# Eight columns of one tile for the index of late V rows, in place of two buffers, in a decoder trunk with PEER layers

## The chip, the cores and the metric

The kernel runs on one core of one Trainium2 chip. The metric is the device time of one execution in microseconds; before the change it is 3107.72 us, the median of three runs (3106.04 to 3110.53). Engines are named as in the profile: PE is TensorE (PEld its weight loads), DVE is VectorE, ACT is ScalarE, POOL is GpSimd, SP is SyncE.

## The reference

Four decoder layers over 256 tokens of width 1024. Each layer is a token mixer (HGRN2, FoX attention, Mamba-2 SSD, HGRN2) followed by a PEER feed-forward layer, and each adds to the residual stream. The part around the change is the PEER layer, which picks 16 of 16384 single-neuron experts for each token and each of 8 heads:

```python
def peer_ffn(h, w_q, sub_keys, u_tab, v_tab):
    ...
    idx = jnp.take_along_axis(cand_i, pos, axis=-1)     # 16 experts per token and head
    gates = jax.nn.softmax(top_s, axis=-1)
    u = jnp.take(u_tab, idx, axis=0)
    v = jnp.take(v_tab, idx, axis=0)
    act = jax.nn.gelu(jnp.einsum('md,mhkd->mhk', xb, u), approximate=False) * gates
    return jnp.einsum('mhk,mhkd->md', act, v)
```

So each expert costs a row of U (4 KB), a dot product with the token, a GELU, and a row of V (4 KB) that is added with the weight `act`.

## The kernel before

**Stages and steps.** Tokens are handled in blocks of 128, so there are 8 stages (4 layers, 2 blocks). A stage has 64 steps, one for each of 8 heads and 8 pairs of experts; the 512 steps of the program are counted by `i`. One step takes two experts of each of the block's 128 tokens, in two groups of 128 rows: group `g` = 0 is the first 64 tokens, group 1 the other 64. Beside the steps of stage s runs, spread over them as background work, all that stage s+1 needs first: its norm, its mixer's projections, its queries and scores (`side`, `products_`, `others`), and the routing of the heads to come (`route_steps`). The order on every engine is that in which the code is written; nothing is reordered.

**A step's transfers.** All are indirect DMAs that POOL issues, on one queue, with 128 row numbers each, a column of an int32 tile:
- `fetch(i, 0)` (L1588) brings the U and V rows of group 0, 8 KB each, 1 MB in all, into one of four buffers.
- `fetch(i, 1)` (L1588) brings the U rows of group 1 alone, 0.5 MB, into one of three buffers.
- `rest_of(i)` (L1600) brings the V rows of group 1 later, 0.5 MB into another three buffers, and only for tokens whose GELU is not exactly zero: row numbers beyond the table are left out by `bounds_check`. These are the late V rows.

The row numbers of the late V rows are made by DVE in `ask(i)`: one operation sets a large offset where the GELU is zero, and the next writes the column `w` of 128 int32 numbers, the tile `ask`. That tile had two buffers used in turn, so `ask(i)` writes where `ask(i-2)` wrote, and may do so only when the DMA `rest_of(i-2)` has read its row numbers; what the program waits for is that DMA's end.

**A step's order.** In step i, POOL issues `fetch(i+2, 1)`, `rest_of(i-1)` and `fetch(i+3, 0)` (a little apart from this at the ends of stages). DVE does `dot(i, 0)` and `dot(i, 1)` (the scalar_tensor_tensor of 128x1024 with a sum), then DVE's share of the background work, then `ask(i)`, then routing and more background work. ACT does the GELUs and the 64-column diagonals `dg` and `dh`, by which PE weighs the rows. PE's `add_rows` (L1668) in step i adds first the late V rows of step i-3, with `dh`, then the V rows of group 0 of step i, with `dg`; behind them stand the background matmuls (L258, L262).

**Who frees what.** `fetch(i+4, 0)` needs the buffer that `dot(i, 0)` and `add_rows` of (i, 0) have read. `fetch(i+3, 1)` needs that of `dot(i, 1)`. `rest_of(i)` needs the numbers of `ask(i)` and the buffer that `add_rows` of step i-3 has read. Besides, the software DMAs use eight semaphores in turn (DMASW0 to DMASW7), and each DMA waits until the one eight before it has landed. SP issues the weights' loads (L412, 1 MB each, on a queue of its own), partly into the two buffers of the tile `raw`.

Helpers: every DVE operation carries L219 or its own line, ACT's carry L232, matmuls L258, transposes L262; the trace's groups are therefore told apart by their tiles.

Of the kernel before, what the change touches and what calls it, by code (L numbers as in the profile page):

```python
# [12 lines left out]
I32 = mybir.dt.int32  # L13
# [6 lines left out]
P = 128  # L20
# [160 lines left out]
def trunk(ctx: ExitStack, tc: tile.TileContext, d: dict, out: bass.AP):  # L181
    nc = tc.nc
    SB = bass.MemoryType.PSUM
    cpool = ctx.enter_context(tc.tile_pool(name="c", bufs=1))
    rawp = ctx.enter_context(tc.tile_pool(name="raw", bufs=NRAW))
    wk2 = ctx.enter_context(tc.tile_pool(name="wk2", bufs=2))
# [58 lines left out]
    small = cpool.tile([P, 2], F32, name="eps")  # L245
    eps, spare = small[:, 0:1], small[:, 1:2]
    trimask = cpool.tile([P, P], U8, name="trimask")
    m64 = cpool.tile([P, 64], F32, name="m64")

    pe = [0.0]  # L250
# [104 lines left out]
    for l in range(DEPTH):  # L355
# [9 lines left out]
        for u in ours:  # L365
            t, _, i, where, again = kept[u]
# [1193 lines left out]
    acts = {}  # L1560
    accs = {}
    asks = {}
# [28 lines left out]
    def ask(i):  # L1591

        s, hh, q = pairs[i]
        a, w = acts[i], asks.setdefault(i, wk2.tile([P, 1], I32, name="ask", bufs=2))
        vec.tensor_scalar(a[:, 5:6], a[:, 3:4], 0.0, float(FAR), op0=OP.is_equal, op1=OP.mult)
        stt(w, a[:, 5:6], 1.0, got[s, hh][1][:, 1, 0, q:q + 1], op0=OP.add, op1=OP.add)

# [188 lines left out]
    for s in range(STAGES):  # L1786
# [23 lines left out]
        for i in range(64 * s, 64 * s + 64):  # L1810
# [21 lines left out]
            if i < CLOSE:  # L1832
                ask(i)
# [34 lines left out]
```

## Time and profile before

| | |
|---|---|
| median of three runs | 3107.72 us (3106.04 to 3110.53) |
| the profiled execution, its own time | 3110.88 us |
| its span | 3109.1 us |
| mean granted TensorE clock | 0.969 |
| busy share of the span: PE, DVE, POOL, ACT | 88%, 71%, 56%, 49% |
| bytes moved by DMA | 1235.74 MB, mean 397 GB/s |

The span is from the first to the last instruction of the profiled execution; 1.8 us of its own time lie around it. A row of the page's fifth part tells line, engine, operation, tiles written and read and the count, then the busy time, the mean of one in ns, and the engine's idle time just before with what ended it. In the view of windows, a row gives for a stretch of time the busy us of each engine (with its instructions), the granted clock, the mean busy share of the 16 DMA engines, and the GB/s; the DMA share goes a little over 1 where packets of an engine overlap. In the view of waits, a row names who waited, after `<-` who ended the wait, then the total in us, the number of waits and the longest.

### The profile page before, as it was taken

The numbers are of one execution on the slowest core, as the hardware profiler recorded it, in microseconds if no ns is written. First come the engines' busy times: TensorE is split into PE (matmuls) and PEld (weight loads), VectorE is DVE, ScalarE is ACT, GpSimd is POOL, SyncE is SP. The second block draws the span as 40 slices with busy tenths as digits, with TensorE's granted clock in tenths as the row PEclk, the third lists the DMA queues.
The fourth block names the chain that finished last, engine by engine and source line by source line (L and its number), as shares of the span: only waits on it lengthen the run. The fifth ranks groups of instructions, "written<-read, shape, count | busy, mean of one in ns | idle before, by whom it ended". The sixth has DMA issues, their size and how long they took to land.

```text
span 3109.1 us, 35708 instructions
## 1 busy us (share of the span) xinstructions
PE 2744.5 (88%) x9490; PEld 1110.9 (36%) x9490; DVE 2209.5 (71%) x6666; ACT 1524.9 (49%) x4410; POOL 1735.6 (56%) x1544
## 2 busy tenths in 40 slices
PE   9989897988789888999789999889988899887777
PEld 4434333332235334344233543343323253342111
DVE  1676667767866867888677787678667767787774
ACT  2455444464444644587345675346444545444333
POOL 0365465655656655555465554556546555666664
PEclk9999999999999999999999999999999999999999
DMA  7799999999999999999999999999999999999998
GB/s 310 276 408 391 407 413 413 413 409 402 409 412 414 406 412 412 380 416 411 408 391 387 382 416 415 405 396 391 416 416 407 387 394 416 393 405 397 406 411 345
DMA packets 249463, 1235.74 MB, mean 397 GB/s; under 512 B 35985, under 2 KB 36625, under 8 KB 160560
## 3 DMA queue, kind: packets, MB, share of 16 engines
q0 software_dynamic: 221184, 1039.92, 83.7%
q1 hardware_dynamic: 28080, 193.55, 15.1%
q8 instruction: 78, 1.28, 0.2%
q14 instruction: 121, 0.99, 0.1%
HBM read 1266.23 MB, written 1.05 MB: 408 GB/s over the span
## 4 chain that ended last, share of the span: by engine, by line
DMA 38%; PE 28%; DVE 21%; ACT 7%; issue 5%; POOL 0%; POOLq 0%; DVEq 0%; SPq 0%; ACTq 0%
DMA arena<-in_uv,ask 37%; PE pj L258 13%; PE pj L1668 11%; DVE arena L219 11%; PE ps L258 3%; ACT L232 3%; DVE cs L219 2%; ACT dots L232 1%; DVE si L219 1%; ACT dg L232 1%; DVE ti L219 1%; DVE af L219 1%; DVE gs L219 1%; DVE ts L219 1%; DVE ask L219 1%
## 5 line engine op out<-in xcount | busy, mean ns | idle before, releaser
L1588 POOL DMA_INDIRECT arena<-in_uv,ix x1024 | 1120.3, 1094 | 602.3 <-DVE arena L219 224.2
L219 DVE SCALAR_TENSOR_TENSOR arena<-arena 128x1024 f32<-128x1024 f32 (+3 forms) x1282 | 1285.3, 1043 | 2.8 <-DMA arena<-in_uv,ix 1.4
L1668 PE MATMUL pj<-arena,dg 128*64 128x512 f32 x2048 | 1035.3, 630 | 211.6 <-ACT dg L232 210.0
L1668 PE MATMUL pj<-arena,dh 128*64 128x512 f32 x2048 | 1028.6, 627 | 122.8 <-DMA arena<-in_uv,ask 116.3
L1600 POOL DMA_INDIRECT arena<-in_uv,ask x508 | 606.4, 1194 | 748.6 <-issue 330.5
L232 ACT ACTIVATE dots<-dots 128x1 f32<-128x1 f32 x1024 | 204.7, 200 | 1314.3 <-DVE arena L219 1312.9
L258 PE MATMUL pj<-arena 128*128 128x128 f32 (+1 forms) x1752 | 509.4, 439 | 1.8 <-ACT arena L232 0.8
L1668 PEld LDWEIGHTS pj<-arena,dh 128*64 128x64 f32 x2048 | 247.8, 141 | 652.6 <-issue 491.5
L219 DVE SCALAR_TENSOR_TENSOR ask<-dots,gs 128x1 int32<-128x1 f32 x508 | 81.0, 159 | 561.1 <-DMA arena<-in_uv,ask 551.5
L1668 PEld LDWEIGHTS pj<-arena,dg 128*64 128x64 f32 x2048 | 245.2, 139 | 628.6 <-ACT dg L232 421.1
L232 ACT ACT_TABLE_LOAD x332 | 426.0, 1283 | 6.3 <-DVE arena L219 0.8
L258 PE MATMUL pj<-raw,arena 128*128 128x512 f32 x808 | 387.3, 614 | 10.1 <-DMA raw<-in_ssm 5.1
L258 PEld LDWEIGHTS pj<-arena 128*128 128x128 f32 x1752 | 258.1, 192 | 258.8 <-issue 237.1
L258 PEld LDWEIGHTS pj<-raw,arena 128*128 128x128 f32 x808 | 144.1, 192 | 243.1 <-issue 213.3
L232 ACT ACTIVATE dg<-dg,dots 128x64 f32<-128x64 f32 x512 | 178.1, 348 | 16.6
L232 ACT ACTIVATE dg<-m,gs 128x64 f32<-128x64 f32 x512 | 170.1, 332 | 0.0
L232 ACT ACTIVATE dh<-m,dots 128x64 f32<-128x64 f32 x508 | 168.8, 332 | 1.6 <-PE pj L1668 1.6
L219 DVE TENSOR_SCALAR dots<-dots 128x1 f32<-128x1 f32 x508 | 76.6, 151 | 129.0 <-ACT dots L232 128.7
L232 ACT ACTIVATE dots<-dots,gs 128x1 f32<-128x1 f32 x508 | 149.6, 294 | 16.5
L258 PE MATMUL ps<-arena 128*128 128x128 f32 (+6 forms) x1120 | 147.4, 285 | 3.1 <-ACT arena L1252 1.3
L258 PEld LDWEIGHTS ps<-arena 128*128 128x128 f32 (+3 forms) x1120 | 111.7, 168 | 79.0 <-issue 43.2
L219 DVE DVE_READ_ACCUMULATOR arena<-arena 128x1 f32 x1024 | 83.4, 81 | 0.0
(130 smaller groups left out, 1763.3 us busy)
## 6 DMA issues: line engine op xcount, KB each, us to landing
raw<-in_ssm SPq DMA_DIRECT2D x48, 1024.0 KB, 8.9
raw<-in_hg SPq DMA_DIRECT2D x35, 1024.0 KB, 9.1
arena<-in_wq SPq DMA_DIRECT2D x28, 1024.0 KB, 8.9
arena<-in_hg SPq DMA_DIRECT2D x27, 1024.0 KB, 14.1
arena<-in_uv,ix POOLq DMA_INDIRECT x1028, 9.9
raw<-in_fox SPq DMA_DIRECT2D x14, 1024.0 KB, 9.2
arena<-in_fox SPq DMA_DIRECT2D x9, 1024.0 KB, 12.3
raw<-in_wq SPq DMA_DIRECT2D x8, 1024.0 KB, 9.9
```

The costliest lines, as they stand in the source:

```text
L219: return getattr(nc.vector, name)(o, *a, **k)
L232: nc.scalar.activation(o, i, f, **k)
L258: nc.tensor.matmul(o, w, m, start=start, stop=stop)
L1588: nc.gpsimd.indirect_dma_start(buffer(i, g), None, halved if apart(i, g) else d["uv"], bass.IndirectOffsetOnAxis(ap=got[s, hh][0][:, g, q: ...
L1600: nc.gpsimd.indirect_dma_start(rows(i, 1), None, halved, bass.IndirectOffsetOnAxis(ap=asks.pop(i), axis=0), bounds_check=2 * DEPTH * P * P ...
L1668: nc.tensor.matmul(accs[s][e][g * 64:g * 64 + 64], diags[i, g], rows(i, g)[:, e * 512:(e + 1) * 512], start=False, stop=hh == 7 and q == N ...
```

## The change

The tile `ask` becomes one tile of 128x8 int32 that lives as long as the program, and `ask(i)` writes column i mod 8 of it. `rest_of` is as it was and reads that column.

```diff
--- before.py
+++ after.py
@@ -245,6 +245,7 @@
     small = cpool.tile([P, 2], F32, name="eps")
     eps, spare = small[:, 0:1], small[:, 1:2]
     trimask = cpool.tile([P, P], U8, name="trimask")
+    index_ring = cpool.tile([P, 8], I32, name="ask")
     m64 = cpool.tile([P, 64], F32, name="m64")
 
     pe = [0.0]
@@ -1591,7 +1592,7 @@
     def ask(i):
 
         s, hh, q = pairs[i]
-        a, w = acts[i], asks.setdefault(i, wk2.tile([P, 1], I32, name="ask", bufs=2))
+        a, w = acts[i], asks.setdefault(i, index_ring[:, i % 8:i % 8 + 1])
         vec.tensor_scalar(a[:, 5:6], a[:, 3:4], 0.0, float(FAR), op0=OP.is_equal, op1=OP.mult)
         stt(w, a[:, 5:6], 1.0, got[s, hh][1][:, 1, 0, q:q + 1], op0=OP.add, op1=OP.add)
 
```

The instructions of every engine and their order stay the same; lines below the new one move by one (L1588 is L1589 after, L1600 is L1601). What moves is waits. On DVE, near the end of the last stage (two steps without background work), before:

```order
L219 SCALAR_TENSOR_TENSOR arena,dots<-arena 128x1024 [waits DMASW5_49]
L219 SCALAR_TENSOR_TENSOR arena,dots<-arena 128x1024 [waits DMASW6_49]
L219 TENSOR_SCALAR dots<-dots 128x1 [waits Activation_49]
L219 SCALAR_TENSOR_TENSOR ask<-dots,gs 128x1 [waits DMASW2_49,DVE_49]
L219 SCALAR_TENSOR_TENSOR arena,dots<-arena 128x1024 [waits DMASW0_49]
L219 SCALAR_TENSOR_TENSOR arena,dots<-arena 128x1024 [waits DMASW1_49]
L219 TENSOR_SCALAR dots<-dots 128x1 [waits Activation_49]
L219 SCALAR_TENSOR_TENSOR ask<-dots,gs 128x1 [waits DMASW5_49,DVE_49]
```

and now, at the same place:

```order
L219 SCALAR_TENSOR_TENSOR arena,dots<-arena 128x1024 [waits DMASW5_49]
L219 SCALAR_TENSOR_TENSOR arena,dots<-arena 128x1024 [waits DMASW6_49]
L219 TENSOR_SCALAR dots<-dots 128x1 [waits Activation_49]
L219 SCALAR_TENSOR_TENSOR ask<-dots,gs 128x1 [waits DVE_49]
L219 SCALAR_TENSOR_TENSOR arena,dots<-arena 128x1024 [waits DMASW0_49]
L219 SCALAR_TENSOR_TENSOR arena,dots<-arena 128x1024 [waits DMASW1_49]
L219 TENSOR_SCALAR dots<-dots 128x1 [waits Activation_49]
L219 SCALAR_TENSOR_TENSOR ask<-dots,gs 128x1 [waits DVE_49]
```

The wait for a DMA (here the ones counted by DMASW2 and DMASW5) is gone from `ask`, in 506 of its 508 instructions; the first two never had it. No DVE instruction has a wait that it did not have. In the turn of eight, the two dots behind the first `ask` wait for DMASW0 and DMASW1, the two transfers issued just ahead of the one that `ask` waited for (DMASW2). On POOL, the same place, before:

```order
L1600 DMA arena<-in_uv,ask 128x1024 [waits DMASW2_49,DVE_49,PE_49]
L1588 DMA arena<-in_uv,ix 128x2048 [waits DMASW3_49,PE_49]
L1588 DMA arena<-in_uv,ix 128x1024 [waits DMASW4_49,DVE_49]
L1600 DMA arena<-in_uv,ask 128x1024 [waits DMASW5_49,DVE_49,PE_49]
L1588 DMA arena<-in_uv,ix 128x2048 [waits DMASW6_49,PE_49]
L1588 DMA arena<-in_uv,ix 128x1024 [waits DMASW7_49,DVE_49]
```

and now:

```order
L1601 DMA arena<-in_uv,ask 128x1024 [waits DMASW2_49,DVE_49,PE_49]
L1589 DMA arena<-in_uv,ix 128x2048 [waits DMASW3_49,PE_49]
L1589 DMA arena<-in_uv,ix 128x1024 [waits DMASW4_49,DVE_49]
L1601 DMA arena<-in_uv,ask 128x1024 [waits DMASW5_49,DVE_49,PE_49]
L1589 DMA arena<-in_uv,ix 128x2048 [waits DMASW6_49,PE_49]
L1589 DMA arena<-in_uv,ix 128x1024 [waits DMASW7_49,DVE_49]
```

Nothing moved here but the line numbers: the late V rows still wait for the DMA of the same semaphore eight issues before, for DVE's `ask`, and for PE, which must have read the buffer's last rows. On PE seven waits are named otherwise, at transposes and small matmuls of the mixers; on ACT and SP nothing differs.

## The prediction

> **What bounds the kernel now.** I read the page's DMA part first, then its chain, then windows over the span, then the waits, and last a stretch of the timeline. From the page:
>
> ```profile
> DMA packets 249463, 1235.74 MB, mean 397 GB/s; under 512 B 35985, under 2 KB 36625, under 8 KB 160560
> q0 software_dynamic: 221184, 1039.92, 83.7%
> q1 hardware_dynamic: 28080, 193.55, 15.1%
> ...
> DMA 38%; PE 28%; DVE 21%; ACT 7%; issue 5%; POOL 0%; POOLq 0%; DVEq 0%; SPq 0%; ACTq 0%
> DMA arena<-in_uv,ask 37%; PE pj L258 13%; PE pj L1668 11%; DVE arena L219 11%; PE ps L258 3%; ACT L232 3%; DVE cs L219 2%; ACT dots L232 1%; DVE si L219 1%; ACT dg L232 1%; DVE ti L219 1%; DVE af L219 1%; DVE gs L219 1%; DVE ts L219 1%; DVE ask L219 1%
> ```
>
> The 16 DMA engines are busy 99% of the span (83.7 + 15.1% and a little), and 37% of the chain that ended last runs through the late V rows, whose end lets `ask` go on. These two read differently: the first says that bytes bound the kernel, the second that a loop of waits does. The windows decide between them. Row by row: most of the program, the last steps, a stretch heavy with weights, then the nine stretches between 200 and 3080 us that fall furthest behind.
>
> ```profile
> 110.00:3085.00 2975.00, 2625.42 (x9070) 1050.65 (x9068) 2177.43 (x6589) 1483.93 (x4326) 1730.96 (x1536) 0.97 1.01 404
> ...
> 3000.00:3070.00 70.00, 55.31 (x119) 14.06 (x119) 38.28 (x91) 22.33 (x89) 44.73 (x44) 0.98 1.02 414
> 1900.00:1960.00 60.00, 48.34 (x117) 16.53 (x116) 33.92 (x104) 18.60 (x55) 24.73 (x22) 0.96 1.02 417
> 235.00:265.00 30.00, 30.00 (x167) 18.18 (x166) 23.21 (x70) 14.44 (x48) 17.89 (x17) 1.00 0.97 357
> 1270.00:1315.00 45.00, 45.00 (x154) 18.18 (x154) 40.72 (x136) 27.55 (x79) 26.46 (x23) 1.00 0.95 357
> 1545.00:1585.00 40.00, 38.10 (x125) 14.99 (x124) 28.13 (x86) 16.31 (x53) 23.75 (x23) 0.99 0.97 368
> 1625.00:1665.00 40.00, 33.52 (x138) 13.08 (x135) 31.39 (x89) 21.06 (x64) 24.89 (x23) 0.96 0.94 352
> 1715.00:1755.00 40.00, 40.00 (x221) 24.36 (x218) 26.48 (x86) 17.50 (x58) 20.68 (x18) 0.94 0.94 350
> 2075.00:2120.00 45.00, 43.48 (x133) 17.11 (x130) 37.92 (x108) 32.79 (x82) 30.01 (x25) 0.96 0.94 350
> 2410.00:2450.00 40.00, 32.62 (x94) 11.11 (x93) 33.96 (x97) 20.95 (x60) 25.47 (x22) 0.96 0.96 359
> 2495.00:2530.00 35.00, 35.00 (x209) 21.68 (x207) 19.62 (x47) 17.61 (x57) 21.95 (x20) 1.00 0.98 379
> 2670.00:2712.00 42.00, 40.16 (x124) 14.24 (x124) 29.10 (x84) 18.95 (x65) 26.92 (x25) 0.96 0.98 376
> ```
>
> In the last steps, where nothing but the steps themselves runs, the DMA engines do 414 GB/s at a share of 1.02, and with weights beside them 417. Over 2975 us the mean is 404 GB/s. If all of it went at 414, 2975 x (1 - 404/414) = 72 us would go: that is the room for any change that moves no byte less. Counted by the share instead, 2975 x (1 - 1.01/1.02) = 29 us. The nine stretches last 357 us and hold 46 us of it by GB/s (for each, its length x (1 - GB/s / 414): 4.1, 6.2, 4.4, 6.0, 6.2, 7.0, 5.3, 3.0, 3.9). In seven of them PE is busy 95% or more; in two (1625 and 2410) it is 84 and 82%, and DVE 78 and 85%. So the kernel is bound by bytes nearly everywhere, and by PE or DVE in short stretches in which the queue runs low.
>
> The waits, in total:
>
> ```profile
> DVE ask L219 <- DMA arena<-in_uv,ask: 551.5, 253, 8.1
> ...
> POOL arena L1600 <- issue: 330.5, 196, 8.3
> POOL arena L1600 <- PE pj L1668: 240.6, 238, 6.6
> ...
> PE pj L1668 <- ACT dg L232: 210.0, 149, 3.2
> ```
>
> DVE's longest wait is the one that the change takes away: 253 times, 2.2 us each. The timeline near the end shows a step in that state:
>
> ```profile
> 3068.66 0.16 DVE L219 SCALAR_TENSOR_TENSOR ask<-dots,gs 128x1 int32<-128x1 f32 x1 [2.02 <-DMA arena<-in_uv,ask]
> 3068.70 1.90 PE L1668 MATMUL pj<-arena,dh 128*64 128x512 f32 x4 [1.03 <-DMA arena<-in_uv,ask]
> 3068.74 1.22 DVE L219 SCALAR_TENSOR_TENSOR arena<-arena 128x1024 f32<-128x1024 f32 x1
> 3069.59 1.24 POOL L1600 DMA_INDIRECT arena<-in_uv,ask  x1 [1.15 <-issue]
> ...
> 3073.70 0.16 DVE L219 SCALAR_TENSOR_TENSOR ask<-dots,gs 128x1 int32<-128x1 f32 x1 [2.17 <-DMA arena<-in_uv,ask]
> ...
> 3079.96 0.16 DVE L219 SCALAR_TENSOR_TENSOR ask<-dots,gs 128x1 int32<-128x1 f32 x1 [3.38 <-DMA arena<-in_uv,ask]
> ...
> 3080.89 1.30 POOL L1600 DMA_INDIRECT arena<-in_uv,ask  x1 [0.49 <-DVE ix L219]
> ```
>
> The late rows of two steps ago land; DVE's `ask` and PE's `add_rows` are let go at once; POOL issues the next late rows 0.93 us after `ask` began (3069.59 - 3068.66). The step takes 5.04 us (3073.70 - 3068.66), which is 2 MB at 414 GB/s: the wait is the queue's back pressure, felt on DVE.
>
> **The change part by part.** No instruction comes, goes or moves; 506 waits go, and no DVE or POOL instruction gains one. The writing of a column of eight in place of a column of one is the same 128x1 write, so I cost it at nothing; were each of the 508 rows of `ask` (0.16 us above) half as long again, that is 41 us of DVE, which has 2975 - 2177 = 798 us free there.
>
> *In the stretches bound by bytes* (all but some 400 us) the wait goes and its time doesn't. What is late next: the two dots wait for the transfers of DMASW0 and DMASW1, issued just ahead of the one that `ask` waited for (DMASW2). A transfer of 128x1024 f32 is 0.52 MB, 1.27 us at 414 GB/s, so DVE is held again at most 1.3 us earlier in the queue, plus the work that stood between. On POOL, the late rows then wait for the DMA eight before, two transfers ahead of the old one (2.5 us), so with the 0.93 us they can be issued up to 3.4 us earlier, and the fetches behind them too: 3.4 us x 414 GB/s = 1.4 MB more lie in the queue. The engines move the same bytes at the same rate; gain 0.
>
> *Where DVE lets the queue run low* (1625 and 2410), that deeper queue lasts 3.4 us longer. Each stretch loses more than that (6.0 and 5.3), so 2 x 3.4 = 6.8 us come back. This is an upper value if the stretch before it was not in the waiting state.
>
> *Where PE does* (the seven others), late rows hang on PE's `add_rows`, not on `ask` (the row of 240.6 us). PE gains only what it gets ahead beforehand: its wait for `dg`, 210.0 us in 149 times, 1.4 us each, which ends earlier because the dot behind `ask` starts earlier. That wait isn't there before every stretch (149 of 512 steps), so I take half: 7 x 0.7 = 4.9 us; bounds 0 and 7 x 3.4 = 23.8.
>
> *The small dips elsewhere* hold 72 - 46 = 26 us by GB/s, but part of that is the rate of skipped and short rows, which no wait explains; I take a tenth, 2.6 us, bounds 0 and 13 (half).
>
> *The end.* The last late rows are issued at 3080.89, after an `ask` that waited 3.38 us. Everything after that is a tail of add, norm and store. Issued earlier, they still lie behind other transfers; I take 2 us, bounds 0 and 3.4.
>
> *The start*, up to 110 us, has no `ask`: 0.
>
> Sum: 6.8 + 4.9 + 2.6 + 2 = 16.3 us, on the profiled execution 3110.9 - 16.3 = 3094.6; the median of the runs is 3.2 us below that execution, so 3107.7 - 16.3, or 3091 us (0.5% less). The upper bounds together give 6.8 + 23.8 + 13 + 3.4 = 47 us; all of them at once is unlikely.
>
> [...]
>
> **The rivals.**
>
> *No change (within 0.2%, 6.2 us).* The stretches are PE's, PE gains no lead, and the two of DVE are entered without a lead: only the end and some dips remain, 2 to 5 us, 3104 us. For it: seven of nine stretches have PE at 95% or more. Against: the 210 us of `dg` waits stand on PE.
>
> *A deeper queue is also faster.* At 417 GB/s where weights lie beside the V rows and 414 where they don't, more bytes in flight may raise the rate: 2975 x 404 x (1/414 - 1/417) = 20.9 us beyond the forecast, 3107.7 - 16.3 - 20.9 = 3070 us. Against: those are larger, contiguous rows. [...] The trace shows no window above 417.
>
> *Slower: the weights come late.* With 1.4 MB more of V rows ahead, a weight load that shares the engines lands up to 3.4 us later. The rows of the tile `raw`, through which most weights pass:
>
> ```profile
> L412 SPq DMA_DIRECT2D raw<-in_ssm x48: 327/328/430, 1204.7 to 1929.7; - x48
> L412 SPq DMA_DIRECT2D raw<-in_hg x35: 327/328/430, 27.1 to 2629.9; - x35
> L412 SPq DMA_DIRECT2D raw<-in_fox x14: 327/328/443, 478.5 to 1058.3; - x14
> L412 SPq DMA_DIRECT2D raw<-in_wq x8: 328/375/432, 100.1 to 2637.5; - x8
> ...
>   DMA raw<-in_ssm: 11.4, 11
> ...
>   DMA raw<-in_hg: 5.7, 3
> ...
> DMA to landing us min/median/max: 7.1/9.1/26.7
> ```
>
> PE and its weight loads wait for them 17.1 us in 14 places, so they come just in time there; there are 105 loads (48, 35, 14, 8). It decides from the point at which loads in PE's seven stretches (277 us of 2975, so about 10 of the 105) and in as many dense places again are late by the whole 3.4 us: 20 x 3.4 = 68 us less the 16.3, which is 52 us slower, 3159 us. If it is only those 14 places, 14 x 3.4 = 48 us, less 16.3: 3139 us. Against: PE, not DMA, sets the pace there, and the V rows' queue moves 83.7 of the 99% before the change too, so a load shares the engines with it already. [...]
>
> That the waits stay is excluded: the built order shows them gone.
>
> **How the numbers follow.** Forecast 0.61, at 3091 us; no change 0.22, at 3104; deeper and faster 0.11, at 3070; slower 0.06, at 3139. Two runs of this kernel differ by up to 0.14% (3106.04 to 3110.53), so about 0.2% can be told. The forecast itself reaches from 3079 (dips and PE stretches at half their bounds: 6.8 + 11.9 + 6.5 + 3.4 = 28.6) to 3101 (DVE's stretches alone). With most of the case of no change above and the half of the fast case below, the range is 3074 to 3106. Faster 0.61 + 0.11 = 0.72, same 0.22, slower 0.06.
>
> **What would show it.** Right: the wait of `ask` for the late rows gone from DVE; a new wait of the dots on `arena<-in_uv,ix`, far below 551.5 us; late rows issued earlier against the landing before them; the GB/s of 3000 to 3070 unchanged near 414, those of 1625 and 2410 up, those with PE at 100% up less. Wrong: the nine stretches as low as before (no lead was carried in), 417 or more in the last steps (depth makes speed), or PE's waits for `raw` grown from 17 us to 50 or more (weights late). The forecast's own step most likely to fail is the 3.4 us of lead: it needs POOL to be free to issue and PE to have read the buffer.

## The result, and the profile after

The changed kernel takes 3076.74 us (median of 6 runs, 3073.28 to 3080.45), the kernel before 3106.88 us beside it (6 runs, 3102.78 to 3110.78): a ratio of 0.9904, 95% interval 0.9891 to 0.9917, or 30.1 us less. The profiled execution took 3075.86 us; its span of 3074.1 us is 35.0 us shorter than that of before. The forecast was 16.3 us less, so the sign was right and the size about half. Measured again beside later experiments, the change gave 0.9905 (0.9889 to 0.9922).

From the page of the changed kernel, its DMA line and its chain:

```profile
DMA packets 249460, 1235.72 MB, mean 402 GB/s; under 512 B 35985, under 2 KB 36625, under 8 KB 160560
...
DMA 43%; PE 28%; DVE 16%; ACT 3%; issue 3%; POOL 1%; POOLq 0%; DVEq 0%; ACTq 0%
DMA arena<-in_uv,ix 23%; DMA arena<-in_uv,ask 21%; PE pj L1669 12%; PE pj L259 12%; DVE arena L219 9%; PE ps L259 3%; DVE cs L219 1%; ACT L232 1%; ACT dots L232 1%; PE ps L263 1%; DVE ti L219 1%; DVE si L219 1%; DVE ts L219 1%; DVE ask L219 1%; DVE sv L219 1%
```

The bytes are the same. The chain has 5 points more of DMA and 5 less of DVE, the late V rows (`ask`) have 16 points less, and the first fetches (`ix`) have 23, where they had at most 1.

The same windows as before, in the order most of the program, last steps, stretch with weights, nine stretches; the stretches are placed where the same steps run now, 5 to 30 us earlier, and the last steps 35 us earlier. After a window and its length stand the busy us of PE, PEld, DVE, ACT and POOL, then the granted clock, the DMA share and the GB/s:

```profile
110.00:3050.00 2940.00, 2406.96 (x9062) 1049.18 (x9061) 2218.12 (x6586) 1484.45 (x4323) 1749.17 (x1536) 0.92 1.01 409
2965.00:3035.00 70.00, 40.69 (x115) 13.98 (x112) 40.57 (x87) 21.90 (x86) 47.25 (x43) 0.78 1.02 414
1900.00:1960.00 60.00, 38.69 (x103) 15.28 (x104) 34.15 (x91) 20.42 (x65) 30.17 (x26) 0.80 1.02 416
230.00:258.00 28.00, 28.00 (x156) 16.70 (x155) 22.89 (x66) 13.76 (x46) 16.89 (x15) 1.00 1.02 413
1262.00:1306.00 44.00, 44.00 (x139) 17.05 (x136) 41.25 (x140) 28.08 (x81) 27.52 (x24) 1.00 0.97 357
1534.00:1574.00 40.00, 37.96 (x118) 14.42 (x116) 29.03 (x89) 16.82 (x53) 25.28 (x25) 1.00 1.00 393
1610.00:1650.00 40.00, 33.28 (x117) 11.94 (x114) 33.93 (x94) 22.57 (x70) 26.28 (x24) 1.00 0.96 372
1696.00:1736.00 40.00, 40.00 (x224) 24.00 (x221) 27.92 (x90) 18.49 (x60) 21.88 (x19) 0.97 0.99 389
2054.00:2098.00 44.00, 42.49 (x129) 16.62 (x128) 37.87 (x109) 32.58 (x77) 30.49 (x26) 1.00 1.00 385
2385.00:2425.00 40.00, 32.97 (x94) 11.59 (x93) 31.80 (x93) 23.32 (x64) 24.82 (x23) 0.96 0.98 380
2467.00:2502.00 35.00, 35.00 (x221) 22.63 (x219) 20.86 (x55) 16.73 (x52) 23.58 (x21) 1.00 1.02 413
2640.00:2681.00 41.00, 37.93 (x131) 14.84 (x131) 29.87 (x85) 15.72 (x57) 27.33 (x25) 1.00 1.02 409
```

Where bytes bind, nothing moved: 414 GB/s in the last steps, as before, and 416 beside the weights, where it was 417. In the stretches much came back. By the measure of the prediction, length x (1 - GB/s / 414), the room in the nine is now 0.1, 6.1, 2.0, 4.1, 2.4, 3.1, 3.3, 0.1 and 0.5, in sum 21.6 us where it was 46.0. The room of the whole row is 2940 x (1 - 409/414) = 35.5 us where it was 71.9. So of 36.4 us that came back, 24.4 did in the nine stretches and 12 elsewhere. (Window edges are whole us, so a single stretch is good to about 1 us; the GB/s of the whole row are whole numbers, so the 12 is good to some 5.)

The waits of the changed kernel:

```profile
PE pj L1669 <- DMA arena<-in_uv,ask: 451.2, 224, 9.7
DVE arena L219 <- DMA arena<-in_uv,ix: 440.2, 256, 5.4
...
POOL arena L1601 <- PE pj L1669: 257.2, 205, 5.0
...
POOL arena L1601 <- DMA arena<-in_uv,ix: 153.8, 92, 4.1
...
POOL arena L1589 <- DVE arena L219: 93.8, 131, 3.8
...
PE pj L1669 <- ACT dg L232: 39.6, 28, 2.8
```

The 551.5 us of `ask` are gone, and the dots wait 440.2 us for their own rows instead. PE waits 39.6 us for the diagonal `dg` where it waited 210.0, and 451.2 us for the late V rows themselves (116.3 before), which come when the queue has brought them.

What this does to a step is seen near 1510 us, in two neighbouring steps (236 before, 237 now), in each of which PE had to wait for late rows. Before:

```profile
1513.21 0.16 DVE L219 SCALAR_TENSOR_TENSOR ask<-dots,gs 128x1 int32<-128x1 f32 x1 [5.99 <-DMA arena<-in_uv,ask]
...
1513.26 1.90 PE L1668 MATMUL pj<-arena,dh 128*64 128x512 f32 x4 [1.37 <-DMA arena<-in_uv,ask]
...
1515.12 1.21 DVE L219 SCALAR_TENSOR_TENSOR arena<-arena 128x1024 f32<-128x1024 f32 x1
...
1516.60 0.35 ACT L232 ACTIVATE dg<-dg,dots 128x64 f32<-128x64 f32 x1
...
1517.00 1.93 PE L1668 MATMUL pj<-arena,dg 128*64 128x512 f32 x4 [1.84 <-ACT dg L232]
```

And now:

```profile
1507.25 1.21 DVE L219 SCALAR_TENSOR_TENSOR arena<-arena 128x1024 f32<-128x1024 f32 x1
...
1508.73 0.35 ACT L232 ACTIVATE dg<-dg,dots 128x64 f32<-128x64 f32 x1
...
1509.84 0.61 PE L1669 MATMUL pj<-arena,dh 128*64 128x512 f32 x1 [1.42 <-DMA arena<-in_uv,ask]
1509.96 0.61 PE L1669 MATMUL pj<-arena,dg 128*64 128x512 f32 x1
...
1511.27 0.59 PE L1669 MATMUL pj<-arena,dg 128*64 128x512 f32 x1
```

Before, the landing (1513.2) let DVE go; the first dot came 1.9 us later, ACT's `dg` after it, and PE added the late rows (1.90 us), sat idle 1.84 us, and added group 0 (1.93 us): done at 1518.93, 5.7 us after the landing. Now the dot and `dg` are done when the rows land, and PE runs both additions at once: done at 1511.86, 2.0 us after the landing. The two write different halves of the accumulator's partitions. In these rows they run beside each other: started 0.12 us apart, the eight matmuls take 2.02 us (1511.86 - 1509.84), where four took 1.90 and 1.93. That the halves are what lets them, no run shows.

Over the program, the busy time in `add_rows` alone, PE's and then PEld's, of before and of after (in the view of windows, restricted to that line):

```profile
0.00:3109.10 3109.10, 1548.11 (x4096) 420.79 (x4096) 0.97 0.99 397
```

```profile
0.00:3074.10 3074.10, 1320.11 (x4096) 414.76 (x4096) 0.93 1.00 402
```

By the groups of before, `dg` took 1035.3 us and `dh` 1028.6:

```profile
L1668 PE MATMUL pj<-arena,dg 128*64 128x512 f32 x2048 | 1035.3, 630 | 211.6 <-ACT dg L232 210.0
L1668 PE MATMUL pj<-arena,dh 128*64 128x512 f32 x2048 | 1028.6, 627 | 122.8 <-DMA arena<-in_uv,ask 116.3 <-ACT dh L232 6.2
```

So 1035.3 + 1028.6 - 1548.1 = 516 us of them ran beside each other. After, the groups `dg` and `dh` take 1126.6 and 1122.3 us, and 1126.6 + 1122.3 - 1320.1 = 929 us do.

### The profile page after: what moved, and what is told of

The parts are those of the page before. It is cut to its first block, busy times and chain, and to the rows that moved or that the text cites. A ratio compares the mean times of both kernels' runs of the same rounds, so it can differ in the third digit from the quotient of the medians.

```text
span 3074.1 us, 35204 instructions
## 1 busy us (share of the span) xinstructions
PE 2525.9 (82%) x9490; PEld 1109.9 (36%) x9490; DVE 2250.9 (73%) x6666; ACT 1526.2 (50%) x4410; POOL 1755.1 (57%) x1544
## 4 chain that ended last, share of the span: by engine, by line
DMA 43%; PE 28%; DVE 16%; ACT 3%; issue 3%; POOL 1%; POOLq 0%; DVEq 0%; ACTq 0%
DMA arena<-in_uv,ix 23%; DMA arena<-in_uv,ask 21%; PE pj L1669 12%; PE pj L259 12%; DVE arena L219 9%; PE ps L259 3%; DVE cs L219 1%; ACT L232 1%; ACT dots L232 1%; PE ps L263 1%; DVE ti L219 1%; DVE si L219 1%; DVE ts L219 1%; DVE ask L219 1%; DVE sv L219 1%
## 5 line engine op out<-in xcount | busy, mean ns | idle before, releaser
L219 DVE SCALAR_TENSOR_TENSOR arena<-arena 128x1024 f32<-128x1024 f32 (+3 forms) x1282 | 1305.5, 1046 | 449.5 <-DMA arena<-in_uv,ix 440.2
L1669 PE MATMUL pj<-arena,dh 128*64 128x512 f32 x2048 | 1122.3, 676 | 497.0 <-DMA arena<-in_uv,ask 451.2
L1589 POOL DMA_INDIRECT arena<-in_uv,ix x1024 | 1089.7, 1064 | 640.1 <-issue 160.2
L1669 PE MATMUL pj<-arena,dg 128*64 128x512 f32 x2048 | 1126.6, 678 | 31.7 <-ACT dg L232 31.5
L1601 POOL DMA_INDIRECT arena<-in_uv,ask x508 | 656.4, 1292 | 657.9 <-PE pj L1669 257.2
L1669 PEld LDWEIGHTS pj<-arena,dh 128*64 128x64 f32 x2048 | 260.6, 148 | 1078.7 <-issue 515.4
L1669 PEld LDWEIGHTS pj<-arena,dg 128*64 128x64 f32 x2048 | 261.4, 149 | 165.6 <-issue 81.5
L219 DVE MAX8 sv<-arena 128x8 f32<-128x128 f32 x256 | 61.3, 280 | 31.5 <-ACT arena L1239 17.9
```

What stands on the lines that cost most here:

```text
L219: return getattr(nc.vector, name)(o, *a, **k)
L1589: nc.gpsimd.indirect_dma_start(buffer(i, g), None, halved if apart(i, g) else d["uv"], bass.IndirectOffsetOnAxis(ap=got[s, hh][0][:, g, q: ...
L1601: nc.gpsimd.indirect_dma_start(rows(i, 1), None, halved, bass.IndirectOffsetOnAxis(ap=asks.pop(i), axis=0), bounds_check=2 * DEPTH * P * P ...
L1669: nc.tensor.matmul(accs[s][e][g * 64:g * 64 + 64], diags[i, g], rows(i, g)[:, e * 512:(e + 1) * 512], start=False, stop=hh == 7 and q == N ...
```

## The experiments

The theory of the prediction was a deeper queue of V rows (POOL issues earlier), with a little lead for PE beside it. The rivals to be told from it: that the column layout itself matters; that the gain is in proportion to the wait removed, wherever it stood; and that it is DVE's own lead that counts, and not POOL's. All ratios are to the kernel before on the same chip; the diffs are against the changed kernel.

**Two columns and three.**

```diff
-index_ring[:, i % 8:i % 8 + 1]
+index_ring[:, i % 2:i % 2 + 1]      # e1; in e2: i % 3
```

> The index columns lie in one tile, but only two of its columns are used in turn, so that ask(i) waits for rest_of(i-2) again (506 waits are back). Theory (the gain is a lead: with the wait gone, DVE and POOL run ahead and the queue is deeper when PE or DVE slow down): the wait is all there was to it, so the time of the kernel before, ratio 0.998 to 1.002, and the wait of ask for the late rows near 550 us again. Rival (the columns of one tile that is never released, in place of buffers of a pool, matter by themselves): faster than before, ratio 0.990 to 0.997.

> Three columns in turn in place of eight: ask(i) waits for rest_of(i-3), which the buffer of the late rows waits for on POOL anyway. Lead theory: that wait is one transfer (1.3 us) behind what the dots of the same step waited for, so little stands in its way: ratio 0.989 to 0.993, as with eight, and a small wait of ask, under 60 us. Rival (DVE profits from being able to run several steps ahead): only part of the gain, ratio 0.994 to 0.998.

Measured: two columns 1.0002 (0.999 to 1.0014), three 0.9907 (0.9881 to 0.9932). The wait of `ask` with two columns, then with three:

```profile
DVE ask L219 <- DMA arena<-in_uv,ask: 536.9, 242, 8.4
```

```profile
DVE ask L219 <- DMA arena<-in_uv,ask: 34.8, 34, 2.2
```

One tile with two columns is the kernel before again, so the layout costs and gives nothing and the wait is all. A third column takes the wait down to 34.8 us and gives the whole gain.

**Where the wait matters.** Eight columns only in the 159 steps around and ahead of the stretches (e3), or only in the others (e4).

```diff
+NEAR = ((8, 26), (187, 207), (228, 276), (313, 333), (372, 404), (414, 435))
+n = 8 if any(a <= i < b for a, b in NEAR) else 2      # e4: 2 and 8 swapped
-index_ring[:, i % 8:i % 8 + 1]
+index_ring[:, i % n:i % n + 1]
```

> Eight columns only in 159 of the 508 steps, namely in those of the nine stretches in which the DMA rate is low and some 10 steps ahead of each; two columns in the other 349. Lead theory: nearly the whole gain, 24 to 31 us, ratio 0.990 to 0.9925, since the lead is built up in a few steps and is used in these stretches alone. Rival (each wait that goes saves a little, in proportion to the waits taken away): these steps hold 166 of the 561 us of DVE's waits at ask, so 9 us, ratio 0.997.

> The opposite: eight columns in the 349 steps far from the nine stretches, two columns in the 159 steps in and ahead of them. Lead theory: the lead that is built up is lost at the first ask with a wait and isn't there in the stretches; what is left is the small dips and the end, 2 to 8 us, ratio 0.9975 to 0.9995. Rival (in proportion to the waits taken away): these steps hold 395 of the 561 us of waits, so 21 us, ratio 0.993.

Measured: near 0.9925 (0.9898 to 0.9952), far 0.9984 (0.9973 to 0.9996). The shares of the wait in these expectations were wrong: added up by step, the trace of before has 135.8 us of the 551.5 in the near steps and 415.7 in the others, so a gain in proportion would have been 7.4 us near (0.9976) and 22.7 us far (0.9927). The runs show the reverse, 23 us and 5 us. What was left of the wait, near and far:

```profile
DVE ask L220 <- DMA arena<-in_uv,ask: 399.5, 181, 7.6
```

```profile
DVE ask L220 <- DMA arena<-in_uv,ask: 146.5, 58, 7.8
```

399.5 us of the wait may stay and three quarters of the gain are there. What a wait is worth is decided by the stretch it stands in or ahead of. Less busy time of PE alone decides as little: its busy time in `add_rows` is 1498.7 us with the near steps free and 1390.5 with the far ones (1548.1 before), and the run that saves more of it gains less.

**Whose lead: DVE's or POOL's.** A clearing of the column that the late rows of step i-2 were fetched by waits for their landing. It is put on DVE behind `ask` (e5), or on POOL ahead of the late rows' issue (e7); e6 and e8 clear a column that is long free, so nothing waits.

```diff
 stt(w, a[:, 5:6], 1.0, got[s, hh][1][:, 1, 0, q:q + 1], op0=OP.add, op1=OP.add)
+k = (i + 6) % 8                                # e6: (i + 2) % 8, e8: (i + 4) % 8
+nc.vector.memset(index_ring[:, k:k + 1], 0)    # e7, e8: nc.gpsimd, in rest_of
```

> Eight columns, but right behind ask(i) DVE clears the column of step i-2, which it may do only when rest_of(i-2) has landed: the late rows of step i can be asked for early, and DVE is held where it was held before. It splits the lead in two. If the gain comes from the late rows being issued earlier by themselves, most of it stays: ratio 0.990 to 0.994. If it comes from DVE running ahead (its dots free the buffers of the next fetches, its diagonals' inputs come earlier), it is gone: 0.998 to 1.002. I expect the second more than the first, 0.995 to 0.999, since the fetches behind the late rows still hang on the dots. The 508 added clears cost DVE some 0.1 us each, 50 us, of which next to nothing is on the path; the next run has them too.

> The same 508 clears on DVE, but of the column of step i-6, whose DMA has long landed: no wait. It prices the added instruction. Both theories: as with the change alone, ratio 0.989 to 0.993.

> Eight columns, and POOL clears the column of step i-2 right ahead of the issue of the late rows of step i: POOL waits there until rest_of(i-2) has landed, DVE doesn't. If the depth of the queue is what the gain comes from, it is mostly gone: POOL can't issue earlier than before, at most 5 or 6 transfers are in flight, ratio 0.996 to 1.000. If DVE's (and PE's) own lead is what counts, whatever lies in the queue, it mostly stays: 0.990 to 0.994. I expect between them, 0.993 to 0.997.

> The same 508 clears on POOL, but of the column of step i-4, which has landed: no wait. It prices the added instruction on POOL, some 0.1 to 0.3 us each beside 3.4 us of POOL's work in a step of 6 us. Both theories: ratio 0.989 to 0.994.

Measured: DVE held 1.0004 (0.9991 to 1.0018), its control 0.9925 (0.9906 to 0.9945); POOL held 0.9925 (0.9905 to 0.9945), its control 0.9932 (0.9913 to 0.9951). Both held runs were expected in between (0.995 to 0.999 and 0.993 to 0.997); each came out at its end instead. PE's wait for `dg` with DVE held, and two waits with POOL held:

```profile
PE pj L1671 <- ACT dg L232: 202.9, 153, 3.0
```

```profile
POOL ask L1602 <- DMA arena<-in_uv,ask: 459.3, 316, 8.5
...
PE pj L1671 <- ACT dg L232: 48.2, 40, 2.8
```

POOL may wait 459.3 us for the landing that `ask` waited for, and nothing is lost. Hold DVE there, and all is. The time from issue to landing of the late rows shows how deep the queue was, before, after and with POOL held:

```profile
DMA to landing us min/median/max: 4.9/8.8/23.4
```

```profile
DMA to landing us min/median/max: 5.3/11.4/28.0
```

```profile
DMA to landing us min/median/max: 4.8/9.1/22.3
```

At 414 GB/s, 11.4 - 8.8 = 2.6 us more are, as an estimate, 1.1 MB more in the queue in the changed kernel, near the 1.4 MB of the prediction. But with POOL held the queue is nearly as shallow as before (0.3 us more), and the gain is there; with both dots held, below, it is deeper (a median of 10.6 us), and most of the gain is not. The deeper queue came with the change and did not make the gain.

**Which of DVE's work.** The same clearing, of the column of step i-3 (the landing that `ask(i-1)` waited for), placed ahead of the two dots, behind them, or between them. With them the changed kernel ran once more (e11).

```diff
+if 3 <= i < CLOSE + 3:
+    k = (i - 3) % 8
+    nc.vector.memset(index_ring[:, k:k + 1], 0)
 dot(i, 0)                # e9: as here; e12: behind this line
 ...
 dot(i, 1)                # e10: behind this line
```

> Eight columns, and DVE clears, at the start of each dot(i, 0), the column that the late rows of step i-3 were fetched by: DVE may start the two dots of a step only when those rows have landed. It is the landing that the kernel before waits for in ask(i-1), but here the background work of DVE that stands between ask(i-1) and dot(i, 0) goes ahead of the wait. Theory A (the gain comes of the dots themselves being early: U buffers come free earlier, ACT's diagonals are made earlier, PE is not held by them): the whole gain goes, ratio to the kernel before 0.999 to 1.001, PE's wait for dg back near 200 us. Theory B (the gain comes of the background work of DVE that is done in the waiting time): the gain of the same clearing without a wait, 0.9925, stays to at least two thirds, 0.995 or less.

> The same clearing of the column of step i-3, but behind dot(i, 1): the two dots of step i (2.4 us of DVE) go ahead of the landing that they waited for, and everything of DVE behind them waits for it. Theory A (the dots' lead): 2.4 us of work taken out of the wait gives most of the gain back, 0.9945 or less, and PE's wait for dg is well under 100 us. Theory B (the background's): DVE's background work still waits once in each step for the late rows, only for others, so the gain is small, 0.997 or more.

> The changed kernel itself, beside the two others on the same chip: 0.9904 of the kernel before by the first measurement, 0.9890 to 0.9920 here. Both theories expect the same of it; it shows how far e9 and e10 stand from it, and with the clearing without a wait (0.9925 and 0.9932) what 508 idle clearings cost.

> The same clearing of the column of step i-3, now between dot(i, 0) and dot(i, 1): the first dot of the step, and with it ACT's diagonal dg, goes ahead of the landing of those late rows; the second dot, which frees the buffer that fetch(i+3, 1) needs, waits for it. Theory C (what counts is dg, which PE needs as soon as the late rows have landed): the whole gain stays, 0.9940 or less, PE's wait for dg stays near 40 us as in the changed kernel. Theory D (what counts is the second dot, by the buffer that it frees for POOL's next fetch): most of the gain goes, 0.9960 or more, although dg is early, and POOL's fetches wait for DVE's dots some 200 us or more, as in the kernel before (224 us) and with both dots held (280 us). A figure between 0.9940 and 0.9960 leaves the two apart by halves.

| the landing is waited for | ratio (95% interval) | PE busy in `add_rows`, us |
|---|---|---|
| behind DVE's background, in `ask` (before) | 1 | 1548 |
| ahead of both dots (e9) | 0.9981 (0.9971 to 0.9990) | 1557 |
| between the dots (e12) | 0.9951 (0.9933 to 0.9969) | 1394 |
| behind both dots (e10) | 0.9922 (0.9906 to 0.9939) | 1321 |
| nowhere (e11) | 0.9905 (0.9889 to 0.9922) | 1330 |

The waits, of both dots held, of the second one held, and of the wait behind both. DVE's wait at the clearing stands mostly beside it, as `issue` (idle time for which the profile shows no reason), at an instruction whose row starts some 0.02 us ahead of the clearing's; the control e6 has no `issue` wait on DVE.

```profile
DVE arena L219 <- issue: 488.9, 231, 7.5
...
POOL arena L1589 <- DVE arena L219: 280.4, 232, 4.7
...
PE pj L1672 <- ACT dg L232: 108.2, 96, 8.0
```

```profile
DVE arena L219 <- issue: 351.3, 200, 6.7
...
POOL arena L1589 <- DVE arena L219: 286.0, 283, 4.5
...
PE pj L1669 <- ACT dg L232: 65.1, 58, 3.3
```

```profile
DVE arena L219 <- DMA arena<-in_uv,ix: 379.0, 244, 3.4
...
POOL arena L1589 <- DVE arena L219: 44.4, 56, 2.7
...
PE pj L1669 <- ACT dg L232: 38.2, 30, 3.0
...
DVE dots L219 <- issue: 23.0, 9, 3.5
...
DVE arena L219 <- issue: 18.2, 14, 2.5
```

With both dots held, 0.0019 of the gain is left: that is the background work of DVE done in the waiting time, about a fifth. Theory A fits best, though not to the letter: the whole gain was to go, and PE's wait for `dg` came to 108 us, not 200. With the first dot free half of the gain is there, and with both free all that the controls with a clearing show (0.9925 and 0.9932). In the last case little is left of the wait itself (11.9 us at the clearings and 23.0 + 18.2 us of `issue` beside them, where both dots held have 9.1 and 488.9): by the time a step's dots are done, the late rows of three steps ago have mostly landed. The second dot held gave 0.9951, between C and D: `dg` counts, and so does something behind the second dot. POOL's fetches wait 286.0 us for the dots in that run, 224.2 before and 93.8 after, which would fit the buffer that the second dot frees. The run with POOL held speaks against it: there too the fetches stood behind the landing of the late rows (459.3 us), and the gain stayed. What behind the second dot makes the other half is open; no run took POOL's wait for the dots away alone.

## Why the prediction was right, and where its size was wrong

*The edit costs nothing, only the wait goes.* Right: `ask` took 159 ns before and 160 after, and two columns of one tile gave 1.0002.

*Where bytes bind, the time doesn't move.* Right: 414 GB/s before and after in the last steps. The gain was put at 0 there, and the rows agree; the 30.1 us are time in which the 16 engines had too little to do (in the nine stretches their share was 0.94 to 0.98, and is 0.96 to 1.02).

*The new wait of the dots is far below 551.5.* Wrong: 440.2 us. The step was "DVE is held again at most 1.3 us earlier in the queue". That may hold for the queue, but where bytes set the pace an engine's idle time is the span less its work. DVE's was 3109.1 - 2209.5 = 899.6 us and is 3074.1 - 2250.9 = 823.2. It fell by the 35.0 us of the span and by 41.4 us that the same 6666 instructions were busy longer, no more. That most of the wait had to come back could have been seen beforehand; why DVE is busy longer, no run shows.

*1.4 MB more in the queue, which last 3.4 us longer where DVE sets the pace: 6.8 us.* The depth came (1.1 MB), the two stretches gave 11.3 - 7.3 = 4.0 us, but depth wasn't the cause: POOL held undid most of the depth and kept the gain, DVE held undid the gain. This step is the one that failed as a mechanism.

*Seven stretches of PE: 7 x 0.7 = 4.9 us.* Mis-sized, and most of the miss: they gave 34.7 - 14.2 = 20.5 us, 2.9 each, four times the 0.7 and near the upper bound of 23.8. The mechanism (PE's lead, by `dg` earlier) is borne out by the runs with DVE and the dots held. What the term left out is in the step at 1513: a late `dg` costs PE not only the 1.84 us of idle time but 1.81 us more of work (1.90 + 1.93 for 2.02), since additions that could run side by side run one after the other. The halving for "not before every stretch" is the smaller part: without it the term would have been 9.8 us. The prediction also had the stretches with PE at 100% gain less than the others; of those four, 235, 1715 and 2495 went to 413, 389 and 413 GB/s, and only 1270 stayed at 357. That entering a stretch with its V rows added sooner is what PE's lead consists of is read from these rows; no run kept `dg` early and the additions apart.

*Dips elsewhere: 2.6 us, at most 13.* They gave 25.8 - 13.9 = 12 us, good to some 5, close to the bound; which dips, no run tells. *The end: 2 us.* From the last issue of late rows to the end it was 3109.1 - 3080.9 = 28.2 us, and is 3074.1 - 3047.8 = 26.3 in this profile, but 3079.1 - 3051.1 = 28.0 in the second one of the same kernel: between 0 and 2.

*The rivals.* No change is excluded by the interval. A queue that is faster when deeper is refuted: 414 and 416 GB/s, not 417 or more, at 1.1 MB more. The weights did not come late: the waits for `raw` are 10.8 us in 11 places where they were 17.1 in 14. The conditions named for a wrong forecast did not occur; of the nine stretches only 1270 stayed as low as before.

So the forecast's 16.3 us were mainly 6.8 of depth that wasn't the cause, and 4.9 of lead that was worth four times as much. That the time still fell inside the range was luck in part: the forecast's own terms reached down to 3079, the measured 3076.74 lies below, and the range went on to 3074 only for half of the case of a faster queue, which the runs refute.

## What to carry to other kernels

A wait that moves no byte can still cost time if it holds the engine whose results feed the matmuls of the same step (the waits of `ask` on DVE cost 30.1 us, the same landing waited for on POOL, 459.3 us in all, came with 0.9925 beside 0.9932 without a wait): look at what that engine does next and who needs it when the data lands, and price the lead in the stretches where another engine, not the transfers, sets the pace. Where two groups of matmuls can run side by side, a late operand costs the idle time and the overlap too (1.84 and 1.81 us in the step at 1513). And before counting a wait as won, subtract: in a kernel bound by bytes, the idle time of every engine is the span less its work, so most of a wait that is removed can come back at the next instruction that needs data (here 440.2 of 551.5 us).

## What was not expected of the hardware

PE does the same work in less busy time, 2525.9 us for 2744.5, and its granted clock falls: 0.926 over the span for 0.969, and in the last steps 0.78 for 0.98. There PE's work comes in short bursts with idle time between (40.69 us busy of 70, where it was 55.31), and the granted clock changes inside a burst:

```profile
3035.50 0.61 PE L1669 MATMUL pj<-arena,dh 128*64 128x512 f32 x1 [2.86 <-DMA arena<-in_uv,ask]
...
3036.42 1.06 PE L1669 MATMUL pj<-arena,dh 128*64 128x512 f32 x1
```

0.61 us, and 1.06 us less than a microsecond later, a factor of 1.7. In the view of windows the granted clock is 1.00 from 3035.5 to 3036.0 us and 0.50 from 3036.5 to 3037.0. The idle time ahead of this burst was 2.86 us, and the burst's first matmul still took 0.61 us; what sets the clock, no run shows. Where it would matter it didn't fall so far: in seven of the nine stretches the clock is 1.00, in the others 0.97 and 0.96.

Then, 508 clearings of 128x1 that wait for nothing, 59 ns each on DVE (30.0 us in all, which has 823 us free), came with 0.9925 where the kernel without them had 0.9904 and 0.9905. The intervals overlap, so whether they cost the 6 us is open.
